# Second feed-forward stage of an encoder layer: three plain pairs instead of four, groups of 3, 6, 6 and 7 columns, and low parts made by DMA

## Chip, core and metric

The kernel runs on one core of one Trainium2 chip. The core has five engines that run their own instruction streams: TensorE (PE in the profile; its weight loads are shown apart as PEld), VectorE (DVE), ScalarE (ACT), GpSimd (POOL) and SyncE (SP). DMA transfers are issued from the queues of SP, ACT and POOL. The metric is the device time of one execution in microseconds, lower is better.

## What is computed

One layer of an encoder on x of shape 512 x 1024, in float32: a half-step SwiGLU, a mixer (Fourier groups beside attention), a second half-step SwiGLU, a final norm.

```python
def swiglu(h, w_gate, w_up, w_down):
    return (jax.nn.silu(h @ w_gate) * (h @ w_up)) @ w_down
...
x = x + 0.5 * swiglu(rms_norm(x, ffn1_norm), ffn1_w_gate, ffn1_w_up, ffn1_w_down)
...
x = x + jnp.concatenate([f_out, a_out], axis=-1) @ w_out
x = x + 0.5 * swiglu(rms_norm(x, ffn2_norm), ffn2_w_gate, ffn2_w_up, ffn2_w_down)
return rms_norm(x, final_norm)
```

The inner width of both SwiGLUs is 2752: 21 blocks of 128 and a tail of 64. The change lies in the second one alone.

## The kernel before

**Precision.** TensorE multiplies in a rounded 32-bit format. To keep float32 accuracy, every operand is split into a high part (rounded, made by ACT) and a low part (what rounding left, made by DVE: `lows`, L71-72), and every product is three matmuls: high x high, high x low, low x high (`product`, L108-111).

**Layout.** x lies transposed, 8 blocks of 128 channels by 512 positions. A "pair" j is a block of 128 gate columns and the same block of up columns of the weights. A "column" is one of the two; column 2j is pair j's gate, 2j + 1 its up. The tail, 64 of each, is one column by itself ("t", column 42).

**Two ways to make a pair.** A *plain* pair (`gate`) is two columns, each 8 channel blocks x 3 matmuls of 128 x 512, 48 in all. It runs on the unscaled h; the norm's factor is multiplied in when the result is taken from PSUM (`evacuate`). A *seven* (`seven`) uses a Winograd scheme with halves of the channels, of the positions, and of gate and up: seven products of quarter size in place of eight. One pair is then 7 x 4 x 3 = 84 matmuls of 128 x 256. It needs sums and differences of weight quarters (`prepare`) and of h quarters (`operands`, made once per stage into `rt`, in four parts), again with high and low parts.

**Groups.** The pairs of a stage are made and used up in groups (L28). The first group holds the plain pairs and the tail. For each group, eight output chunks d follow: `down` multiplies the group's activations with the down weights into a PSUM bank, `residual` adds the bank to x. The sevens of a group run one pair ahead: while group g's sevens run, the first pair of group g+1 is made as well, and the last pair of the first group is evacuated after the first chunk has started (`rest`). There are seven places for activations (`at`). In the last group of stage two, the last three chunks are taken in two halves of the positions (`closing`), so that norm, scaling and output of the first half run beside the matmuls of the second.

**Order.** TensorE's and SP's instructions stand in the order in which the code issues them (`in_order`). The order on ACT, DVE and POOL is drawn up by a scheduler; each engine works through its own queue strictly in that order.

**Buffers.** In the plain columns, high and low parts lie in `ring` slots and, lent for that time, in two free places of `at`: six slots, three columns at a time. Slots whose first columns alone are rewritten are let go as soon as those columns have been read. Raw weights are loaded by SP into three `raw` tiles.

**Low parts by DMA.** `rest_by_dma` (L90-93) makes a low part in another way: ACT writes minus the high part into the low tile, and a DMA from POOL's queue adds the source to it, from DRAM for weights, from the tile b for h. In stage one (`n_` is 0), the plain columns after the opening and the parts 2 and 3 of h are made so; in stage two (`n_` is 2) DVE makes all.

```python
    def rest_by_dma(lo, hi, src):
        nc.scalar.activation(lo, asf(hi), AF.Copy, scale=-1.0)
        nc.gpsimd.dma_start(out=lo, in_=src, accum_op=ALU.add)
```

**Start of stage two.** Columns 0 and 1 and the tail column come first, then the columns left, 2 to 7, one `gate` call each. Between them stand the evacuations that are due and the four calls of `operands` (L440-455).

Of the kernel before, what the change touches and what calls it, by code (L numbers as in the profile page):

```python
# [16 lines left out]
KD = D // P  # L17
# [7 lines left out]
FILL_LEAD = 0.1  # L25
NS = 12

GROUPS = ((0, "t", 1, 2), range(3, 9), range(9, 15), range(15, 21))  # L28
PLACES = 7
HALF = S // 2  # L30
USES = "a11", "a12", "s1", "s2", "s4", "s3", "a22"
# [11 lines left out]
def encoder(ctx, tc, A, out):  # L43
# [8 lines left out]
    def bank(name):  # L52
        return pp.tile([P, S], F32, tag="bank", name=name)
# [10 lines left out]
    def in_order():  # L64
        return tc.manual_schedule(engines={mybir.EngineType.PE, mybir.EngineType.SP})
# [5 lines left out]
    def lows(lo, src, hi):  # L71
        nc.vector.tensor_tensor(out=lo, in0=src, in1=asf(hi), op=ALU.subtract)  # L72
# [17 lines left out]
# [5 lines that stand above are left out]
    def weights(src, name, n=KD, raw=None, by_dma=False):  # L95
        raw = raw or raw_tile(src, name, n)
        hi, lo = weight_slots()
        if name in HI_DVE:
            nc.vector.tensor_copy(hi[:, :n, :], raw[:, :n, :])
        else:  # L100
            nc.scalar.copy(hi[:, :n, :], raw[:, :n, :])  # L101
        if by_dma:
            rest_by_dma(lo, hi, src)
        else:
            lows(lo[:, :n, :], raw[:, :n, :], hi[:, :n, :])
        return hi, lo

    def product(ps, whi, wlo, mhi, mlo, first, last):  # L108
        nc.tensor.matmul(ps, whi, mhi, start=first, stop=False)  # L109
        nc.tensor.matmul(ps, whi, mlo, start=False, stop=False)  # L110
        nc.tensor.matmul(ps, wlo, mhi, start=False, stop=last)  # L111
# [93 lines left out]
            nc.scalar.copy(self.rb[:, t], pss[1][:, t])  # L205
            return pss[0]

    def ffn(norm, after, wgu, wd, wdt, opening, closing):

        n_ = norm.n
        n_plain = len(GROUPS[0])
        with tc.tile_pool(name=f"act{n_}", bufs=1) as ap, tc.tile_pool(name=f"sums{n_}", bufs=2) as sp:
            at = ap.tile([P, PLACES, 2, S], F32R, name=f"at{n_}")
            rt = ap.tile([P, 7, 2, KH, HALF], F32R, name=f"rt{n_}")
# [3 lines left out]
            def place(j):  # L221
                where[j] = free.pop(0)
                return where[j]
# [3 lines left out]
            def gate(c, between={}, by_dma=False):  # L227
                whi, wlo = weights(wgu[c], f"gu{n_}_{c}", by_dma=by_dma)
                ps = bank(f"gu{n_}_{c}")
                for k in range(KD):  # L230
                    between.get(k, int)()
                    product(ps, whi[:, k, :], wlo[:, k, :], hh[k], hl[k], k == 0, k == KD - 1)
                return ps
# [18 lines left out]
            def operands(rp, i0, i1):  # L252
                for i in range(i0, i1):
                    b = sp.tile([P, 4, HALF], F32, tag="raw_g", name=f"b{n_}_{i}")
                    for o, k in ((0, i), (2, i + KH)):
                        nc.vector.scalar_tensor_tensor(
                            out=b[:, o : o + 2].rearrange("p a b -> p (a b)"), in0=x[k],
                            scalar=gains[:, norm.n, k : k + 1], in1=rp, op0=ALU.mult, op1=ALU.mult,
                        )
                    b12, b11, b22, b21 = (b[:, o] for o in range(4))  # L260
                    t = sp.tile([P, 4, HALF], F32, tag=("s12", "s34")[i % 2], bufs=1, name=f"t{n_}_{i}")
                    for o, (p, q) in enumerate(((b12, b11), (b22, t[:, 0]), (b22, b12), (b21, t[:, 1]))):
                        nc.vector.tensor_tensor(out=t[:, o], in0=p, in1=q, op=ALU.subtract)
                    for src, c in ((b[:, 1:], slice(0, 3)), (t, slice(3, 7))):
                        h, l = rt[:, c, 0, i], rt[:, c, 1, i]
                        nc.scalar.copy(h, src)
                        if src is t or i < 2 or n_:
                            lows(l, src, h)
                        else:
                            rest_by_dma(l, h, src)  # L270

            def back(ts):
                plain[:] = [t for t in plain if all(t is not q for q in ts)]
# [149 lines left out]
            def residual(d, ps, t):  # L423
                nc.vector.scalar_tensor_tensor(  # L424
                    out=x[d][:, t], in0=ps[:, t], scalar=0.5, in1=x[d][:, t], op0=ALU.mult, op1=ALU.add
                )

            every = slice(0, S)
            for gi, group in enumerate(GROUPS):
                last = gi == len(GROUPS) - 1  # L430
                ahead = []
                if gi:
                    rest = seven(range(group[0] + 1, min(group[-1] + 2, NF)), ready)
                else:
                    lent = [at[:, i].rearrange("p a b -> p (a b)") for i in range(PLACES - 4, PLACES)]
                    plain.extend(lent)
                    row = []
                    pss = dict(enumerate(opening(gate, lambda: norm.column([norm.acc]), lambda: row.append(norm.row()))))
                    back(lent[:2])
                    due, parts, left = [*pss, "t"], list(range(KH)), range(2 * len(pss), 2 * n_plain)  # L440
                    pss["t"] = [gate(2 * NF)]
                    tail_weights()
                    for i, c in enumerate(left):
                        pss.setdefault(c // 2, []).append(gate(c, by_dma=not n_))
                        if due:
                            j = due.pop(0)
                            evacuate(at[:, place(j)], n_, pss[j], norm)
                        if c % 2 and c != left[-1]:
                            due.append(c // 2)
                        while len(parts) * len(left) > (len(left) - 1 - i) * KH:  # L450
                            o = parts.pop(0)
                            operands(row[0], o, o + 1)

                    def rest():
                        evacuate(at[:, place(n_plain - 1)], n_, pss[n_plain - 1], norm)

                def added(d, ps):
                    residual(d, ps, every)
                    if last:
                        (after.sums if closing else after.add)(d)  # L460
                    if ahead:
                        f, *a = ahead.pop(0)
                        f(*a)

                waiting = []
                for d in range(KD):
                    if last and closing and d == KD - 3:
                        closing([(e, down(e, group, gi)) for e in range(d, KD)], residual)
                        break
                    if last and d == KD - 2:  # L470
                        back(lent)
                    ps = bank(f"dn{n_}_{d}_{gi}")
                    steps = down(d, group, gi)(ps, every)
                    for _ in range(len(group) - (last and d < 2)):
                        next(steps)
                    waiting.append((d, ps, steps))
                    if d == 1 and not last:
                        ready = prepare(GROUPS[gi + 1][0] + 1)
                        ahead.extend(ready[1])
                    if d == 0:  # L480
                        rest()
                        if last:

                            lent = slots[KD - 2 : KD]
                            plain[2:2] = lent
                            continue
                    for d_, ps, steps in waiting:
                        for _ in steps:
                            pass
                        added(d_, ps)  # L490
                    waiting = []
                for f, *a in ahead:
                    f(*a)
                if not gi:
                    back(lent)
                free.extend(where[j] for j in group)
# [34 lines left out]
    n0, n1 = Norm(0), Norm(1)  # L531
# [69 lines left out]
        return [pss[0:2], pss[2:4]]  # L601

    with in_order():
        ffn(n0, n1, A["wgu1"], A["wd1"], A["wdt1"], opening1, None)


    n2 = Norm(2)
# [378 lines left out]
    n3 = Norm(3)  # L986

    ready = (2, 3)
# [67 lines left out]
        finish(2, 4, n3.rows)  # L1056

    with in_order():
        ffn(n2, n3, A["wgu2"], A["wd2"], A["wdt2"], lambda gate, column, row: [[gate(0, {KD - 1: column}), gate(1, {3: row})]], closing)


def _order():
# [106 lines left out]
```

## Time and profile before

| | us |
|---|---|
| median of 3 runs | 876.37 |
| lowest and highest | 875.76, 877.21 |
| the profiled execution | 877.47 |
| its span, first to last instruction | 875.7 |
| stage two: first gate to the last matmul of the closing | 522.0 to 865.9 |
| of it, plain columns 2 to 7 | 540.0 to 572.9 |
| the first group's output chunks | 572.9 to 593.4 |
| three blocks of sevens, each with the chunks of its group | 593.4 to 687.1, to 781.0, to 865.9 |
| norm, scaling and output of the last half | 865.9 to 875.7 |

The profile is of one execution. In the lists of it, a row has a start, a length, the engine, the line of the kernel, the operation, output and input by the program's names (buffer numbers left out) and a count; in brackets stands how long the engine had been idle before it and what ended that. A matmul's listed length reaches from its start to its result, so rows of matmuls overlap; the step between starts is what one costs.

The granted clock of TensorE was 0.996 over the whole span.

### The profile page before, as it was taken

What the parts mean: (1) busy time and instruction counts of PE and PEld (TensorE: products, weight loads), DVE (VectorE), ACT (ScalarE), POOL (GpSimd) and SP (SyncE); (2) the same over time, 40 slices, a digit from 0 to 9 for tenths busy, and PEclk for the clock granted to TensorE, in tenths of its full rate; (3) what the DMA queues carried; (4) which work ended last, traced back from release to release, by engine and by line L of the source; (5) the groups of instructions that cost most, each with busy time, mean ns of one, the idle gap of its engine ahead of it and who ended that gap; (6) DMA issues with size and microseconds to landing.
All of it is one profiled execution on the core that took longest, in us unless ns stands there. A gap on an engine that the chain in (4) does not pass through costs nothing.

```text
span 875.7 us, 13587 instructions
## 1 busy us (share of the span) xinstructions
PE 862.0 (98%) x5391; PEld 769.1 (88%) x5391; DVE 640.8 (73%) x1011; ACT 459.0 (52%) x763; POOL 27.8 (3%) x33
## 2 busy tenths in 40 slices
PE   8999999999999999999999999999999999999996
PEld 6788998899989998888888888889998999889986
DVE  7798985488746837699888558987974698559554
ACT  7663664266524644677776445535652366226541
POOL 0110000000000000211000000000000000000001
PEclk9999999999999999999999999999999999999999
DMA  7664322323243113621110224242323232323212
GB/s 263 154 150 149 133 85 73 115 97 120 78 140 108 49 51 109 205 79 43 49 49 25 77 70 142 85 133 97 109 79 127 75 117 99 97 101 104 73 37 97
DMA packets 30609, 88.46 MB, mean 101 GB/s; under 512 B 3665, under 2 KB 8529, under 8 KB 30417
## 3 DMA queue, kind: packets, MB, share of 16 engines
q1 hardware_dynamic: 28304, 82.87, 28.3%
q0 software_dynamic: 1696, 4.20, 2.4%
q8 instruction: 42, 0.69, 0.3%
q10 hardware_dynamic: 544, 0.52, 0.2%
q14 instruction: 23, 0.18, 0.1%
HBM read 83.91 MB, written 2.10 MB: 98 GB/s over the span
## 4 chain that ended last, share of the span: by engine, by line
PE 94%; ACT 2%; DVE 2%; DMA 1%; issue 1%; SPq 0%; POOL 0%; DVEq 0%; ACTq 0%
PE r L338 22%; PE q L338 11%; PE dn L109 8%; PE dn L111 8%; PE dn L110 8%; PE p L338 6%; PE gu L109 3%; PE gu L111 3%; PE gu L110 3%; PE out L109 2%; PE out L111 2%; PE out L110 2%; PE pt L851 1%; PE q L109 1%; PE q L110 1%; PE q L111 1%
## 5 line engine op out<-in xcount | busy, mean ns | idle before, releaser
L338 PE MATMUL r<-rt,ring 128*128 128x256 f32 x1632 | 213.0, 282 | 0.0
L338 PEld LDWEIGHTS r<-rt,ring 128*128 128x128 f32 x1632 | 201.8, 188 | 2.4
L109 PE MATMUL dn<-at,ring 128*128 128x512 f32 x303 | 119.7, 395 | 0.0
L110 PE MATMUL dn<-at,ring 128*128 128x512 f32 x303 | 119.6, 395 | 0.0
L111 PE MATMUL dn<-at,ring 128*128 128x512 f32 x303 | 119.6, 395 | 0.0
L338 PE MATMUL q<-rt,ring 128*128 128x256 f32 x816 | 107.9, 281 | 0.0
L424 DVE SCALAR_TENSOR_TENSOR gx<-dn,gx 128x512 f32<-128x512 f32 x61 | 42.1, 690 | 82.0 <-PE dn L111 82.0
L338 PEld LDWEIGHTS q<-rt,ring 128*128 128x128 f32 x816 | 101.6, 188 | 0.0
L72 DVE TENSOR_TENSOR ring<-s,ring 128x1024 fp32r<-128x1024 f32 x68 | 82.9, 1221 | 17.8 <-PE r L338 10.9
L101 ACT CAST ring<-raw_dn 128x768 fp32r<-128x768 f32 (+1 forms) x59 | 45.5, 775 | 92.9 <-PE dn L110 78.8
L299 ACT CAST ring<-s 128x1024 fp32r<-128x1024 f32 x68 | 71.4, 1050 | 38.1 <-PE r L338 18.4
L111 PEld LDWEIGHTS dn<-at,ring 128*128 128x128 f32 x303 | 56.9, 188 | 13.8 <-DVE ring L72 0.2
L110 PEld LDWEIGHTS dn<-at,ring 128*128 128x128 f32 x303 | 57.0, 188 | 13.1
L109 PEld LDWEIGHTS dn<-at,ring 128*128 128x128 f32 x303 | 56.9, 188 | 13.0
L72 DVE TENSOR_TENSOR ring<-raw_dn,ring 128x768 fp32r<-128x768 f32 (+1 forms) x59 | 51.8, 881 | 7.2 <-ACT ring L101 6.2
L72 DVE TENSOR_TENSOR ring<-raw_g,ring 128x1024 fp32r<-128x1024 f32 x34 | 41.6, 1224 | 17.7 <-PE p L338 10.7
L338 PE MATMUL p<-rt,ring 128*128 128x256 f32 x408 | 54.0, 281 | 0.0
L338 PEld LDWEIGHTS p<-rt,ring 128*128 128x128 f32 x408 | 50.8, 188 | 0.0
L299 ACT CAST ring<-raw_g 128x1024 fp32r<-128x1024 f32 x34 | 35.7, 1049 | 22.2 <-DMA raw_g<-in_wgu 9.0
L308 ACT CAST ring<-raw_u 128x512 fp32r<-128x512 f32 x34 | 21.1, 621 | 39.3 <-PE dn L111 19.9
L383 DVE TENSOR_TENSOR u<-g,u 128x512 f32<-128x512 f32 x34 | 23.4, 688 | 15.9 <-ACT u L382 15.9
L109 PE MATMUL gu<-ring 128*128 128x512 f32 x80 | 31.3, 392 | 0.0
(328 smaller groups left out, 1579.9 us busy)
## 6 DMA issues: line engine op xcount, KB each, us to landing
raw_dn<-in_wd SPq DMA_DIRECT2D x48, 384.0 KB, 3.1
raw_g<-in_wgu SPq DMA_DIRECT2D x34, 512.0 KB, 3.8
raw_u<-in_wgu SPq DMA_DIRECT2D x34, 512.0 KB, 4.4
raw_gu<-in_wgu SPq DMA_DIRECT2D x14, 512.0 KB, 3.5
raw_o<-in_wo SPq DMA_DIRECT2D x8, 512.0 KB, 3.6
raw_dn<-in_wd SPq DMA_DIRECT2D x16, 192.0 KB, 2.4
raw_in<-in_wins SPq DMA_DIRECT2D x6, 512.0 KB, 3.6
raw_f<-in_winf SPq DMA_DIRECT2D x4, 512.0 KB, 3.8
```

Source lines behind the costliest of these rows:

```text
L72: nc.vector.tensor_tensor(out=lo, in0=src, in1=asf(hi), op=ALU.subtract)
L101: nc.scalar.copy(hi[:, :n, :], raw[:, :n, :])
L109: nc.tensor.matmul(ps, whi, mhi, start=first, stop=False)
L110: nc.tensor.matmul(ps, whi, mlo, start=False, stop=False)
L111: nc.tensor.matmul(ps, wlo, mhi, start=False, stop=last)
L299: nc.scalar.copy(hi, src)
L308: nc.scalar.copy(hi, src)
L338: nc.tensor.matmul(ps, a[:, ks], b[:, i], start=first and i == 0 and o == 0, stop=i == KH - 1 and o == 2, skip_group_check=not first,)
L383: nc.vector.tensor_tensor(out=u, in0=b["g"], in1=u, op=ALU.mult)
L424: nc.vector.scalar_tensor_tensor(out=x[d][:, t], in0=ps[:, t], scalar=0.5, in1=x[d][:, t], op0=ALU.mult, op1=ALU.add)
L851: nc.tensor.transpose(pt[:, c * P : (c + 1) * P], prob[t, b, c][:, kc * P : (kc + 1) * P], ident)
```

## The change

The list of groups is now a parameter of `ffn`, with a list for each stage. Stage one keeps its own. In stage two, the first group has pairs 0, t and 1 and makes pair 2 ahead by plain products; pair 3, plain before, is made by a seven. The groups after it are 2 to 7, 8 to 13 and 14 to 20, so the last has seven columns. Both conditions that kept `rest_by_dma` to stage one are dropped: in stage two, the low parts of columns 2 to 5 (gate and up weights of pairs 1 and 2) and of the parts 2 and 3 of h taken from b are made by ACT and DMA instead of DVE.

```diff
-GROUPS = ((0, "t", 1, 2), range(3, 9), range(9, 15), range(15, 21))
+GROUPS1 = ((0, "t", 1, 2), range(3, 9), range(9, 15), range(15, 21))
+GROUPS2 = ((0, "t", 1), range(2, 8), range(8, 14), range(14, 21))
...
-    def ffn(norm, after, wgu, wd, wdt, opening, closing):
+    def ffn(norm, after, wgu, wd, wdt, groups, opening, closing):
...
-        n_plain = len(GROUPS[0])
+        n_plain = len(groups[0])
...
                         nc.scalar.copy(h, src)
-                        if src is t or i < 2 or n_:
+                        if src is t or i < 2:
                             lows(l, src, h)
                         else:
                             rest_by_dma(l, h, src)
...
-            for gi, group in enumerate(GROUPS):
-                last = gi == len(GROUPS) - 1
+            for gi, group in enumerate(groups):
+                last = gi == len(groups) - 1
...
-                        pss.setdefault(c // 2, []).append(gate(c, by_dma=not n_))
+                        pss.setdefault(c // 2, []).append(gate(c, by_dma=True))
...
-                        ready = prepare(GROUPS[gi + 1][0] + 1)
+                        ready = prepare(groups[gi + 1][0] + 1)
...
-        ffn(n0, n1, A["wgu1"], A["wd1"], A["wdt1"], opening1, None)
+        ffn(n0, n1, A["wgu1"], A["wd1"], A["wdt1"], GROUPS1, opening1, None)
...
-        ffn(n2, n3, A["wgu2"], A["wd2"], A["wdt2"], lambda gate, column, row: [[gate(0, {KD - 1: column}), gate(1, {3: row})]], closing)
+        ffn(n2, n3, A["wgu2"], A["wd2"], A["wdt2"], GROUPS2, lambda gate, column, row: [[gate(0, {KD - 1: column}), gate(1, {3: row})]], closing)
```

## The prediction

> **What bounds the kernel now.** I read the page first: busy time, then the chain that ended last.
>
> ```profile
> span 875.7 us, 13587 instructions
> PE 862.0 (98%) x5391; PEld 769.1 (88%) x5391; DVE 640.8 (73%) x1011; ACT 459.0 (52%) x763; POOL 27.8 (3%) x33
> ...
> PE 94%; ACT 2%; DVE 2%; DMA 1%; issue 1%; SPq 0%; POOL 0%; DVEq 0%; ACTq 0%
> ```
>
> TensorE is busy all the time and is 94% of the chain. So the change is worth the TensorE time that it takes out, less any wait that it puts in. Next I cut the second feed-forward stage into stretches (columns: stretch, its length, then busy time and instructions of PE, PEld, DVE, ACT, POOL; granted clock; DMA share; GB/s).
>
> ```profile
> 556.45:567.35 10.90, 10.90 (x50) 9.01 (x48) 9.91 (x19) 5.73 (x8) 0.00 (x0) 1.00 0.31 97
> 567.35:572.94 5.59, 5.59 (x26) 4.52 (x24) 5.39 (x8) 2.60 (x4) 0.00 (x0) 1.00 0.28 105
> 572.94:593.37 20.43, 20.43 (x89) 16.55 (x88) 15.62 (x25) 6.66 (x10) 0.00 (x0) 1.00 0.43 142
> 593.37:652.15 58.78, 58.78 (x494) 58.56 (x492) 50.12 (x72) 35.40 (x61) 0.00 (x0) 1.00 0.29 100
> 781.01:829.82 48.81, 48.81 (x409) 48.59 (x408) 37.57 (x54) 28.08 (x49) 0.00 (x0) 1.00 0.28 88
> ```
>
> The rows are: plain columns 5 and 6 (two columns), plain column 7, the first group's eight output chunks, the first block of sevens (six of them without the last product), the last block (five of them, likewise). PE is busy for every length, at granted clock 1.00: there is no gap to win or to hide in. DVE is nearly full in the plain columns (5.39 of 5.59).
>
> **The change, part by part.** *Pair 3 is no longer plain.* Its columns are 6 and 7: half of 10.90 is 5.45, and 5.59, so 11.04 us of TensorE go. Bounds: two columns at the cheaper price, 10.90, or at the dearer, 11.18.
>
> *One more seven in the last block.* Six against five cost 58.78 - 48.81 = 9.97. The upper bound is the step from one seven to the next where a wait is in it, 10.10 (in the chain, the second product starts at 603.63 and 613.73). I take 9.97, since it is what one more costs a block.
>
> *Output chunks.* Three matmuls per chunk, 24 in all, move from the first group to the last. Out go 24 x 20.43/88 = 5.57. In come 15 whole ones at 0.2331 (in the block before, 126 take the 29.37 from 657.77 to 687.14) = 3.50, and 9 that the closing splits in halves, 18 at 0.119 (twelve take 1.43 in the chain) = 2.14. Together +0.07. Their weights move from 192 KB to 128 KB a chunk and from 384 to 448 KB: the bytes are the same, and SP issues as many loads as before.
>
> *Low parts by DMA.* DVE loses four lows of 1.22 and two of 0.95 for columns 2 to 5 and h, and ACT gains four negations of 1.06 and two of 0.85, POOL six issues (0.88 each for weights, 1.29 for h, from the first stage, where the same lines run). None of it is TensorE's, so its price is nothing as long as the lows land before TensorE asks. What hides them is the plain column before. These are the rows for the first, column 2, and for the same step in the first stage.
>
> ```profile
> 530.95 1.05 ACT L101 CAST ring<-raw_gu 128x1024 fp32r<-128x1024 f32 x1 [0.34 <-ACT wt L246]
> 531.90 0.58 ACT L194 COPY rb<-rp 128x512 f32<-128x512 f32 x1
> ...
> 539.96 0.39 PE L109 MATMUL gu<-ring 128*128 128x512 f32 x1
> 540.19 0.40 PE L110 MATMUL gu<-ring 128*128 128x512 f32 x1
> 540.42 0.39 PE L111 MATMUL gu<-ring 128*128 128x512 f32 x1
> ```
>
> ```profile
> 26.28 1.06 ACT L92 ACTIVATE ring<-ring 128x1024 fp32r<-128x1024 f32 x1
> 27.65 1.11 POOL L93 DMA_DIRECT2D ring<-in_wgu  x1 [1.22 <-ACT ring L92]
> ...
> DMA to landing us min/median/max: 5.2/5.7/7.5
> ```
>
> In the program's order the negation comes after the copy to rb: it starts at 532.43 and ends at 533.49. POOL starts 0.31 after such an end (27.34 to 27.65), at 533.80. Call the landing time x: the low is there at 533.8 + x. L111 is the first to use it, at 540.42, its weight load 0.19 earlier, so 540.2: room up to x = 6.4. Behind the negation on ACT stand the table load, the first silu and the cast of column 3; that column's negation ends near 538.1, POOL issues at 538.4, asked for at 545.7: room 7.3. Column 4 has some 8. Column 5 is the tight one again: ahead of its negation ACT now has the negation for h, a cast of h and a cast of the first output weights, and on POOL the DMA for h is issued first; added up from the rows, ACT ends it at 549.4, POOL issues at 549.7, asked for at 556.7: room 7.0. The median 5.7 fits all of them; 7.5, which one of four weight rows shows (the first, issued while 0.75 of the DMA time was taken; here it is 0.26), does not. I take 0 us; the bounds are 0 and, at 7.5, 1.1 + 0.5 = 1.6. The h lows are asked for only at the first seven, some 20 us later. SP's loads come no later than before: a raw tile is now let go after its cast, where it had to wait for DVE.
>
> The Trainium skill ("DMA: Bandwidth & Descriptors", section Anatomy of one DMA) has for a DMA issued from GpSimd about 2.0 us and bytes over 436 GB/s: 3.2 us here as an estimate. By it no low is ever late; the rows are 2 us and more above it, so I go by them.
>
> *The tail.* The last group has seven columns, so in the closing each half chunk has three more matmuls.
>
> ```profile
> 861.13 0.70 POOL L179 TENSOR_TENSOR r<-ms,mhalf 128x2 f32<-128x2 f32 x1 [332.05 <-DVE ms L172]
> ...
> 861.36 0.42 DVE L424 SCALAR_TENSOR_TENSOR gx<-last,gx 128x256 f32<-128x256 f32 x1 [0.31 <-PE last L111]
> 861.86 0.30 DVE L184 COPY wide<-r 128x256 f32<-128x256 f32 x1
> ...
> 862.22 0.43 PE L192 MATMUL rp<-ident,wide 128*128 128x128 f32 x2
> ```
>
> The transposes at L192 stay at the ninth step, and DVE keeps its order: the residual, then the copy to wide. But the residual now waits for the seventh step instead of the sixth, 0.36 later (861.72), so wide starts near 862.06, is there at 862.36, and TensorE waits about 0.2. Bounds 0 and 0.3. After the last matmul nothing is changed: that residual starts as soon as TensorE is done, as before.
>
> Sum: -11.04 + 9.97 + 0.07 + 0.20 = -0.80 us, on the profiled execution's own 877.47 (span 875.7 and 1.8 around it) 876.7; it is 1.1 above the median of three, 876.37, from which I get **875.6**. With the bounds of the prices 875.1 to 876.5.
>
> **Rivals.** *Late lows, slower.* The place is column 2 and, because column 5's cast waits for column 2's end, column 5 again: the stall is (x - 6.4) + (x - 7.0). For it: only 0.7 us of room, the room is worked out from sums of rows, and the first such DMA in this kernel took 7.5. Also on POOL's queue, larger and mixed loads took up to 9.4 (page, part 6). Against it: the three later ones, 5.2 to 5.7, with DVE full. At 7.5 it is 1.6: 877.2. It becomes slower than before by over 0.2% from x = 8.0; halfway between 7.5 and 9.4, at 8.45, it is 3.5: 879.1.
>
> The Trainium skill ("SBUF — State Buffer", section SBUF: two separate sides) says that DVE in a two-port mode, such as an f32 copy, locks GpSimd out of writing descriptors. As a mechanism here it is this rival: at 533.8 DVE runs the four products b of L256 and subtractions, not copies. At 34.74 such an issue beside them took 0.88 and landed after 5.6, so the trace speaks against it, and its chance is within the rival's.
>
> *DVE in the short first group.* Its chunks shrink from 20.43 to 14.86 us, and DVE's 15.62 there shrinks by only some 1.0 (eight lows of 256 instead of 384 columns). With 2.4 of pair 2's evacuation falling into it, 17.0 against 14.86 could hold up weights of a later chunk by 2.1: 877.7. Against it: about 3 us of that work prepare the second seven, which isn't asked for until 8.6 us into the block.
>
> *More gain, faster.* Three times per block a seven loses some 0.14, because a copy on ACT comes late:
>
> ```profile
> 610.75 2.98 PE r L338 x24
> ...
> 640.92 2.84 PE r L338 x24
> ```
>
> Were these nine waits and the tail's gone, it would be 1.2 + 0.2 more: 874.2. For it: ACT's order around the new groups is drawn up anew. Against it: the same three waits stand in every block of both stages, and nothing eases ACT.
>
> **Chances.** The sum holds 0.47. Late lows with x up to 8.0, 0.08; beyond, 0.24. DVE in the first group 0.05. More gain 0.16. Within 0.2% (1.75 us, about what a measurement of this kernel can tell from no change) lie the first, the mild late lows and the third: same 0.60; slower 0.24, faster 0.16. The range 874.0 to 879.2 holds the faster case and the milder half of the slower.
>
> **What would show it.** PE busy through the plain columns with no gap at the third matmul of columns 2 and 5; 21.9 us for columns 2 to 5, 14.9 for the first chunks, 58.8 for the last block; a wait of 0.2 before L193's transposes. A gap of 1 us or more at a plain column's first low, ended by a DMA of POOL's queue, would prove the sum wrong in favour of late lows; a gap within the first chunks ended by DVE, in favour of the third case; blocks under 58.5, of the fourth.

## The result and the profile after

The changed kernel is slower: 878.21 us (median of 22 runs, 876.46 to 881.31) against 877.41 for the kernel before measured beside it, a ratio of 1.0015 with a 95% interval of 1.0008 to 1.0021. Measured a second time, the same kernel gave 1.0027 (1.0017 to 1.0037). The forecast was a gain of 0.8 us; this is a loss of 0.8, small but clear of the interval. The profiled execution took 879.21, its span is 877.4. Lines of the changed kernel are those of the kernel before plus one from L28 on.

First the page of the changed kernel: span, busy times, and the chain that ended last.

```profile
span 877.4 us, 13713 instructions
PE 861.9 (98%) x5436; PEld 770.7 (88%) x5436; DVE 638.9 (73%) x1012; ACT 467.1 (53%) x776; POOL 34.0 (4%) x39
...
PE 86%; DMA 4%; DVE 3%; ACT 3%; issue 2%; SPq 0%; POOL 0%; DVEq 0%; ACTq 0%; POOLq 0%
```

PE's busy time is what it was (861.9 against 862.0). But PE's share of the chain fell from 94% to 86%: the end now hangs on DMA, DVE and ACT in places. Where, the stretches of stage two show (columns as in the prediction: stretch, length, busy time and count of PE, PEld, DVE, ACT, POOL, granted clock, DMA share, GB/s). The rows are columns 2 and 3, columns 4 and 5, the first chunks, the first block of sevens, the last block.

```profile
539.20:550.62 11.42, 11.20 (x50) 8.93 (x49) 11.33 (x19) 11.25 (x15) 3.03 (x3) 1.00 0.78 136
550.62:561.66 11.04, 11.04 (x50) 9.03 (x48) 8.32 (x14) 7.04 (x11) 1.27 (x1) 1.00 0.91 212
561.66:577.10 15.44, 15.29 (x65) 11.88 (x64) 12.41 (x22) 5.39 (x9) 0.00 (x0) 1.00 0.47 135
577.10:637.56 60.46, 59.17 (x494) 58.62 (x492) 53.56 (x78) 35.80 (x62) 0.00 (x0) 1.00 0.31 106
766.31:825.16 58.85, 58.85 (x493) 58.64 (x492) 45.99 (x66) 34.86 (x60) 0.00 (x0) 1.00 0.29 93
```

The last block, now with six sevens and the next group's none, takes 58.85 where five took 48.81: the added seven costs what it should. The first chunks take 15.44 where 14.86 was forecast, the first block 60.46 instead of 58.78, the four columns together 22.46 where an undisturbed run of them takes 21.94 (the experiment with the tail's column, below).

The opening of the kernel varies by over 2 us between executions (the first block of sevens of stage one begins at 80.25 before, at 79.61 after, and between 77.8 and 80.6 in the runs below), so I compare stage two alone: from the second half of gate column 1 (527.66 before, 526.89 after) to the start of the last matmul (869.40 and 870.62). That is 341.74 before and 343.73 after, 1.99 more. The sum had said 0.80 less. The 2.79 between them are column 2 (0.49), the chunks (0.58), the first block (1.68) and 0.04 elsewhere. Each was read from the matmuls' starts: a step between two of them, less the usual 0.233.

*Column 2.* The rows of PE there, POOL's issue, and the same transfer in the chain.

```profile
539.20 0.39 PE L110 MATMUL gu<-ring 128*128 128x512 f32 x1
539.43 0.40 PE L111 MATMUL gu<-ring 128*128 128x512 f32 x1
540.05 0.50 PE L112 MATMUL gu<-ring 128*128 128x512 f32 x1 [0.22 <-DMA ring<-in_wgu]
```

```profile
532.98 0.93 POOL L94 DMA_DIRECT2D ring<-in_wgu  x1 [4.67 <-ACT ring L93]
...
532.98 7.02 DMA ring<-in_wgu
```

The third matmul, the first to use the low part, starts 0.62 after the second. The transfer was issued 6.22 ahead of the column, as forecast (6.16), but took 7.0 and not the median of 5.7.

*Chunks.* ACT and DVE at the end of the columns and in the first chunks of the changed kernel (in brackets the idle time before, and what ended it).

```profile
558.99 1.05 ACT L300 CAST ring<-raw_g 128x1024 fp32r<-128x1024 f32 x1 [3.25 <-DMA raw_g<-in_wgu]
...
560.07 1.23 DVE L73 TENSOR_TENSOR ring<-raw_g,ring 128x1024 fp32r<-128x1024 f32 x1 [1.84 <-ACT ring L300]
...
566.36 1.22 DVE L73 TENSOR_TENSOR ring<-s,ring 128x1024 fp32r<-128x1024 f32 x1
567.49 0.42 DVE L73 TENSOR_TENSOR ring<-raw_dn,ring 128x256 fp32r<-128x256 f32 x1
567.83 0.68 DVE L425 SCALAR_TENSOR_TENSOR gx<-dn,gx 128x512 f32<-128x512 f32 x1
568.43 1.22 DVE L73 TENSOR_TENSOR ring<-s,ring 128x1024 fp32r<-128x1024 f32 x1
569.56 0.42 DVE L73 TENSOR_TENSOR at<-raw_dn,at 128x256 fp32r<-128x256 f32 x1
```

The weights of the first seven (raw_g) come late, ACT and DVE sit idle for them, and then DVE works without a break to 573.4. In its queue the long low parts of the seven's sums (566.36, 568.43) stand ahead of the low parts of down weights 3 and 4 (567.49, 569.56), and PE's gaps are where these two are used: the matmuls that wait for them start at 567.96 and 570.03.

*First block.* SP's loads of the changed kernel and then DVE and ACT.

```profile
553.33 0.33 SPq L292 DMA_DIRECT2D raw_g<-in_wgu  x1
...
554.69 15.64 SPq L88 DMA_DIRECT2D raw_dn<-in_wd  x6
570.43 0.38 SPq L292 DMA_DIRECT2D raw_g<-in_wgu  x1
571.54 0.33 SPq L292 DMA_DIRECT2D raw_u<-in_wgu  x1
...
583.25 0.33 SPq L292 DMA_DIRECT2D raw_g<-in_wgu  x1
583.63 0.42 SPq L292 DMA_DIRECT2D raw_u<-in_wgu  x1
```

```profile
577.75 0.69 DVE L315 TENSOR_TENSOR s<-raw_u 128x512 f32<-128x512 f32 x1 [3.47 <-DMA raw_u<-in_wgu]
```

```profile
588.06 0.62 ACT L309 CAST ring<-raw_u 128x512 fp32r<-128x512 f32 x1 [3.86 <-DMA raw_u<-in_wgu]
588.59 1.04 ACT L300 CAST ring<-raw_g 128x1024 fp32r<-128x1024 f32 x1
589.53 0.36 ACT L375 COPY u<-r 128x256 f32<-128x256 f32 x1
```

This reads as a relay. SP's queue stands on the loads of down weights, whose tiles come free late; so the second seven's weights are issued at 570.43 and 571.54, and raw_u is there 0.65 after the block has begun (577.75), DVE being idle for 3.47. That sets when the tiles come free for pair 6 (583.25, 583.63), and ACT's cast of its raw_u waits until 588.06. Behind that cast, in ACT's strict order, stands the copy at 589.53 that frees a bank, and PE waits for it 1.2 us: the list of PE's waits gives it.

```profile
PE r L339 <- ACT u L375: 1.2, 1, 1.2
PE gu L112 <- DMA ring<-in_wgu: 0.2, 1, 0.2
```

### The profile page after: what moved, and what is told of

Read it like the earlier page. It is cut to its first block, busy times and chain, and to the rows that moved or that the text cites. A ratio compares the mean times of both kernels' runs of the same rounds, so it can differ in the third digit from the quotient of the medians.

```text
span 877.4 us, 13713 instructions
## 1 busy us (share of the span) xinstructions
PE 861.9 (98%) x5436; PEld 770.7 (88%) x5436; DVE 638.9 (73%) x1012; ACT 467.1 (53%) x776; POOL 34.0 (4%) x39
## 4 chain that ended last, share of the span: by engine, by line
PE 86%; DMA 4%; DVE 3%; ACT 3%; issue 2%; SPq 0%; POOL 0%; DVEq 0%; ACTq 0%; POOLq 0%
PE r L339 21%; PE q L339 10%; PE dn L110 8%; PE dn L111 8%; PE dn L112 8%; PE p L339 5%; DMA raw_u<-in_wgu 2%; PE out L110 2%; PE out L112 2%; PE gu L112 2%; PE out L111 2%; PE gu L111 2%; PE gu L110 2%; PE pt L852 1%; PE q L110 1%
## 5 line engine op out<-in xcount | busy, mean ns | idle before, releaser
L339 PE MATMUL r<-rt,ring 128*128 128x256 f32 x1680 | 219.4, 283 | 1.4 <-ACT u L375 1.2
L339 PEld LDWEIGHTS r<-rt,ring 128*128 128x128 f32 x1680 | 207.7, 188 | 4.2 <-ACT u L375 1.4
L339 PE MATMUL q<-rt,ring 128*128 128x256 f32 x840 | 111.1, 281 | 0.0
L339 PEld LDWEIGHTS q<-rt,ring 128*128 128x128 f32 x840 | 104.6, 188 | 0.0
L73 DVE TENSOR_TENSOR ring<-s,ring 128x1024 fp32r<-128x1024 f32 x70 | 85.4, 1221 | 19.0 <-PE r L339 12.4
L300 ACT CAST ring<-s 128x1024 fp32r<-128x1024 f32 x70 | 73.5, 1050 | 37.5 <-PE r L339 17.2
L102 ACT CAST ring<-raw_dn 128x768 fp32r<-128x768 f32 (+3 forms) x58 | 45.3, 784 | 90.2 <-PE dn L111 74.8
L73 DVE TENSOR_TENSOR ring<-raw_dn,ring 128x768 fp32r<-128x768 f32 (+3 forms) x58 | 51.6, 893 | 6.0 <-ACT ring L102 4.0
L309 ACT CAST ring<-raw_u 128x512 fp32r<-128x512 f32 x35 | 21.7, 621 | 41.5 <-DMA raw_u<-in_wgu 16.9
L846 ACT ACTIVATE e<-s,mx,sc 128x512 f32<-128x512 f32 x32 | 25.1, 786 | 11.4 <-DVE mx L844 11.2
```

What stands on the lines that cost most here:

```text
L300: nc.scalar.copy(hi, src)
L309: nc.scalar.copy(hi, src)
L339: nc.tensor.matmul(ps, a[:, ks], b[:, i], start=first and i == 0 and o == 0, stop=i == KH - 1 and o == 2, skip_group_check=not first,)
L846: nc.scalar.activation(e, ps, AF.Exp, bias=mx, scale=f, accum_out=zs[t][:, c, b : b + 1])
```

## The experiments

Theory at the outset: the terms of TensorE were right, and what went wrong is the low parts by DMA, those of h above all, whose transfers hold the tiles b (one tag with raw_g) and lie beside the first seven's loads. Rivals: the shorter first group by itself is too short for DVE; or only the slow landing at column 2 matters. In each diff a minus line is the changed kernel's.

**Halves of the change.** The new groups with all low parts by DVE (`e1_groups_only`), and the old groups with the low parts by DMA (`e2_dma_only`: one list of groups for both stages again).

```diff
-                        if src is t or i < 2:
+                        if src is t or i < 2 or n_:
...
-                        pss.setdefault(c // 2, []).append(gate(c, by_dma=True))
+                        pss.setdefault(c // 2, []).append(gate(c, by_dma=not n_))
```

> The new groups alone: low parts of columns 2 to 5 and of h stay with VectorE. Theory A (the first output chunks, shortened from 20.4 to 14.9 us, are too short for the preparation of the next sevens, so that weight loads come late and a cast that waits for one holds up ScalarE): VectorE has 6.8 us more to do in the same time, so the waits in the chunks and in the first block grow; +2 to +5 us on the kernel before. Theory B (the accumulating DMAs are what costs: the first lands late, and the tile of h that they hold keeps the first weight load back): without them the change is worth the sum of TensorE's terms, -0.8 us.

> The low parts by DMA alone, in the kernel before with its old groups (columns 2 to 7 and parts 2 and 3 of h). Theory A: only column 2's low is late, some 0.4 us, the chunks still have 20.4 us: 0 to +0.5 us on the kernel before, first block of sevens 58.8 us. Theory B: the lost time is here too: +1.5 to +2.5 us.

Neither half is better than the whole: 1.0068 (1.0056 to 1.0080) and 1.0039 (1.0025 to 1.0053), both more than either theory had allowed for. In the first, the chunks lose 6.5 us. PE's waits there, and two stretches:

```profile
PE dn L112 <- DVE ring L73: 3.1, 1, 3.1
PE dn L110 <- ACT ring L102: 1.4, 1, 1.4
```

```profile
566.80:570.03 3.23, 0.16 (x1) 0.00 (x1) 3.23 (x6) 0.00 (x0) 0.00 (x0) 1.00 0.00 0
570.03:573.49 3.46, 3.46 (x9) 2.72 (x10) 3.04 (x5) 2.54 (x4) 0.00 (x0) 0.52 0.39 114
```

DVE is busy through the whole of PE's wait: without the DMAs the short first group is too short for DVE. So the DMAs are needed by the new groups, and h's and the columns' must not be judged alike. In the second, columns 2 and 6 wait for their low parts, 1.0 and 1.6, with landings of 6.9 to 9.4 (one of h's 4.4) where several are under way together; no block is disturbed but the last, by 0.3.

**Which low parts.** Column 2's by DVE (`e4_col2_dve`), and h's by DVE with the columns' left to DMA (`e8_h_dve`, the first two lines of the diff above).

```diff
-                        pss.setdefault(c // 2, []).append(gate(c, by_dma=True))
+                        pss.setdefault(c // 2, []).append(gate(c, by_dma=not n_ or c > 2))
```

> The changed kernel with the low part of column 2 made by VectorE again, the other three columns and h by DMA. Theory A: only the 0.4 us wait at column 2's third matmul goes, and VectorE is 1.2 us later, so that some of it may come back in the chunks: +0.7 to +1.3 us on the kernel before. Theory B: column 5's low follows column 2's, so both are repaired: -0.3 to +0.3 us.

> The changed kernel with h's low parts by VectorE, columns 2 to 5 by DMA. Theory A (VectorE and the weight loads in a first group that is too short): VectorE has 1.9 us more to do before the chunks, the waits in them grow by about that: +2 to +4 us on the kernel before. Theory B for h (the tile b is held until its DMA lands, 4.4 to 7 us, and the first raw gate weights wait for it): the first load is issued earlier than 24 us before the first seven, the waits in chunks and first block shrink: 0 to +0.6 us.

`e4` has no gap at column 2, but loses 1.8 in the chunks, where DVE is 1.2 later and the first seven's load is issued only at 557.39: 1.0031 (1.0019 to 1.0043), more than either theory had priced. `e8` gives DVE 1.9 more and yet has clean chunks and a clean block (58.83); only column 2 still waits, 0.6: 0.9998 (0.9989 to 1.0007). That seemed to fit the theory. The first seven's loads land in 3.6 and 4.5 us instead of 5.6 and 6.5. The answers on DMA issues, first of the changed kernel, then of `e8` (the last number is us from issue to landing):

```profile
raw_g<-in_wgu SPq DMA_DIRECT2D x1, 512.0 KB, 5.6
raw_u<-in_wgu SPq DMA_DIRECT2D x1, 512.0 KB, 6.5
```

```profile
raw_g<-in_wgu SPq DMA_DIRECT2D x1, 512.0 KB, 3.6
raw_u<-in_wgu SPq DMA_DIRECT2D x1, 512.0 KB, 4.5
```

The Trainium skill ("DMA: Bandwidth & Descriptors", section Queues, rings and completion order) says that each DMA engine serves the queues that have work in turn, a packet at a time; the 2 us that SP's loads lose beside POOL's transfer agree with that.

Yet what these 2 us cost isn't shown. The changed kernel issues raw_g 8.3 us ahead of the first chunk and has it 2.8 ahead; `e8` issues it 6.7 ahead and has it 3.1 ahead. Against the chunks, the slow load is there only 0.3 later.

**Earlier loads.** A third tile for raw_g and b (`e3_third_tile`), paid for with single tiles of `kept`; and these single tiles alone, as a control (`e7_single_kept`).

```diff
-                    b = sp.tile([P, 4, HALF], F32, tag="raw_g", name=f"b{n_}_{i}")
+                    b = sp.tile([P, 4, HALF], F32, tag="raw_g", bufs=3 if n_ else 2, name=f"b{n_}_{i}")
...
-                g = sp.tile([P, KD * P], F32, tag="raw_g", name=f"raw_g{n_}_{j}")
+                g = sp.tile([P, KD * P], F32, tag="raw_g", bufs=3 if n_ else 2, name=f"raw_g{n_}_{j}")
...
-                    t = sp.tile([P, HALF], F32, tag=n, name=f"{n}{n_}_{j}")
+                    t = sp.tile([P, HALF], F32, tag=n, bufs=1 if n_ and n != "u2" else 2, name=f"{n}{n_}_{j}")
```

> The changed kernel with a third tile for raw gate weights (and the tiles b of h) in stage two, paid for by one instead of two buffers for the kept products p1 and p5. Theory A: the loads of the first pairs no longer wait for a tile; the first block of sevens goes from 60.5 to 58.8 us and the first chunks from 15.4 to 14.9: -0.8 to 0 us on the kernel before, some 2 less than the changed kernel. Theory B's first half (column 2's low): only what it does not touch stays, 0.4 us at column 2. If the seven itself or the DMA traffic is what costs: no change from the changed kernel, +1.3.

> A control: the changed kernel with one instead of two buffers for the kept products p1 and p5, and no third tile. If the third tile is what removed the waits, this has them still: first block of sevens 60 us or more, +1 to +2.5 us on the kernel before. If it was the buffers' effect on the schedule, the first block is 58.8.

`e3` issues the first seven's load at 541.39 instead of 553.33, and the stalls of chunks and first block are gone; column 2 still waits 0.24. Its stretches: columns 2 and 3, 4 and 5, chunks, first block (the cut before the chunks lies 0.12 early, in column 5).

```profile
537.92:549.10 11.18, 11.18 (x49) 8.93 (x48) 11.06 (x20) 10.91 (x15) 2.90 (x3) 1.00 1.05 236
549.10:560.02 10.92, 10.92 (x49) 8.95 (x48) 10.29 (x19) 6.89 (x11) 1.43 (x2) 1.00 0.62 114
560.02:574.89 14.87, 14.87 (x67) 12.11 (x66) 13.49 (x23) 5.62 (x10) 0.00 (x0) 1.00 0.56 202
574.89:633.66 58.77, 58.77 (x493) 58.55 (x492) 50.74 (x74) 35.46 (x61) 0.00 (x0) 1.00 0.27 92
```

From its first matmul on, the chunks take 14.75, as in every run without a stall there; the block takes 58.77. Stage two takes 340.96, 0.78 less than before. That this is the forecast sum to 0.02 is in part luck, since the sum had no wait at column 2. The timing, 1.0000 (0.9992 to 1.0009), neither shows nor excludes such a gain. The control keeps the stalls (first block 59.85): 1.0021 (1.0012 to 1.0030).

**What is left.** On top of the third tile, column 2's low part by DVE and the tail column's by DMA (`e5_tail_column`); then also the closing's norm one step later (`e6_later_norm`, run twice).

```diff
-                    pss["t"] = [gate(2 * NF)]
+                    pss["t"] = [gate(2 * NF, by_dma=n_ > 0)]
...
-                if i == 5:
+                if i == 6:
...
-                if i == 9:
+                if i == 10:
```

> The kernel with the third tile, and the low by DMA moved from column 2 to the tail column, which is asked for some 10 us after its cast; VectorE makes column 2's low, so its work is the same. If the first accumulating DMA of a stage lands after 6.8 to 8 us wherever it stands, as all runs so far show, the tail column's is there in time and column 2's wait of 0.25 us goes: no gap in the plain columns, -0.9 to -0.2 us on the kernel before. If what was late at column 2 was its place in ScalarE's order, the same. If the accumulate's time is what counts in sum (traffic), nothing moves against the run with the third tile alone (0.0, interval -0.7 to +0.8).

> The same, and in the closing the norm's column of the first half at step 6 instead of 5 and its rows at step 10 instead of 9. By the prediction's step on the tail, the wait of 0.2 us before the transposes goes and nothing takes its place: the gap at their line falls from 0.29 to 0.12 us between starts, 0.2 us faster than the run before it. If VectorE's six scalings then run past the last matmul, 0.1 to 0.4 slower instead.

> The same kernel as e6_later_norm, on the same chip as the two beside it, to compare them in one call: 0.9989 of before, within 0.9980 to 0.9997.

Stage two takes 340.71 and 340.79 (again: 340.62), with no gap in columns, chunks or blocks. The ratios are 0.9990 (0.9980 to 1.0001), 0.9989 (0.9980 to 0.9997) and 0.9994 (0.9985 to 1.0002). The later norm removes the wait at the transposes (0.14 and 0.12 between starts instead of 0.29), but the timing shows nothing of it: `e5` and `e6` do not differ. In the profiles, up to the last transposes, `e6` is 0.26 and 0.09 shorter than `e5`; 0.34 of the 340.79 are these transposes at a lower clock (last section). The tail column's transfer has nothing that waits for it soon and landed after 5.4 to 5.7. So the first such transfer of a stage isn't slow wherever it stands, as `e5`'s expectation had it; `e4`'s had landed after 5.5 already.

**Does DVE for h replace the third tile?** `e9_no_third_tile` is `e6` without the third tile and with h by DVE; `e10_h_dve_too` keeps the tile.

> e6_later_norm with the third tile and the single kept tiles taken back, and the low parts of h by DVE instead of DMA; the low part of the tail column and of columns 3 to 5 by DMA, of column 2 by DVE. My theory: the third tile and DVE for h cure the same thing (the first weight loads are neither late nor slow), so the time is that of e6: 875.2, ratio to before 0.9985 to 0.9995, no stall in the chunks, first block 58.8. Rival: the third tile gave something of its own, or DVE, with 1.9 us more work per stage and column 2's low as well, is late in the first group's chunks (column 2's low alone cost e4 about 1 us there): 876.2 or more, ratio above 1.0, gaps in the chunks ended by DVE.

> e6_later_norm, third tile kept, but the low parts of h by DVE. My theory: with a third tile the accumulates of h cost TensorE nothing, so taking them away gives nothing: 875.2, within 0.3 of e6. Rival one: they still slow the loads beside them, then it is 0.3 or more faster than e6. Rival two: DVE is nearly full in the columns and its 1.9 us more make it late in the chunks: 0.5 or more slower than e6.

It does not: `e9` loses 1.2 in the chunks, at the low part of a down weight, though h has no DMA and the loads land in 3.6 and 4.6: 1.0009 (1.0000 to 1.0019), with `e6` beside it at 0.9994. So the theory in its first form fell: DVE can be late there without any of h's DMAs. `e10` is 1.0002 (0.9993 to 1.0012), with 0.3 lost in the block, within the timing's reach of `e6`.

**DVE's order against h's DMAs.** `e8` differs from the changed kernel in a second way. Its drawn-up DVE order has the low parts of down weights 3 and 4 ahead of the seven's long ones. Both were separated by writing the order of the first group out by hand: `e11` has h by DMA with the order of `e8`, `e12` h by DVE with the order of the changed kernel. In the string, W is a chunk's weights, p a piece of `prepare`, g a residual.

```diff
+                    with tc.manual_schedule(engines={mybir.EngineType.PE, mybir.EngineType.SP, mybir.EngineType.DVE}):
+                        for a in "p0 p1 p5 p4 W2 p2 g0 W3 g1 p6 W4 p3 g2 W5 g3 p7 W6 g4 W7 g5 g6 g7".split():
```

> The changed kernel, h's low parts by DMA as in it, but in the first group of stage two the order of DVE's work is written out by hand, and it is that of e8_h_dve: the low parts of down weights 3 and 4 stand ahead of the low parts of the first seven's sums, where the changed kernel has them behind. Column 2's wait (about 0.5) and the tail's (0.17) stay. Theory A, the order decides (what e8 cured by moving h back to DVE it cured through another drawn-up order): no stall in the chunks, first block near 58.8, stage two 2.3 shorter than in the changed kernel, some 875.9, ratio 0.999 to 1.0005. Theory B, the accumulates of h decide (they share the DMA engines with the first weight loads): the stalls of 0.6 and 1.7 stay, ratio 1.0010 to 1.0021.

> The mirror of it: e8_h_dve (h's low parts by DVE) with the DVE order of the changed kernel in the first group of stage two. Theory A, the order decides: the stalls in the chunks and the first block come back, 2 or more in all, ratio 1.001 to 1.003. Theory B, the accumulates decide: they stay away, chunks 14.9, first block 58.8, ratio 0.999 to 1.0007.

Time lost in the profiles, chunks / first block:

| | h by DMA | h by DVE |
|---|---|---|
| order of the changed kernel | 0.6 / 1.7, again 1.0 / 1.0 | 1.0 / 0.1 (`e12`) |
| order of `e8` | 0.0 / 1.5, again 0.0 / 1.4 (`e11`) | 0.0 / 0.05 (`e8`) |

Neither theory is the whole. The chunks' loss goes with the order, and in this table the first block's goes with h's DMAs. (`e12` loses a further 0.5 in its second block.) But one load sorts the first block's losses better. It is raw_u of the second seven, issued while the chunks run. Here are all profiles of the new groups with two tiles:

| | raw_u lands, us from the block's start | the block loses |
|---|---|---|
| changed kernel, again | +0.6, -0.1 | 1.7, 1.0 |
| `e11`, again | +0.3, +0.1 | 1.5, 1.4 |
| `e7` | -0.7 | 1.1 |
| `e4` (h by DMA too) | -1.2 | 0.05 |
| `e12`, `e9`, `e8`, `e1` (h by DVE) | -1.6, -1.7, -1.8, -2.1 | 0.1, 0.0, 0.05, 0.1 |

In the first three rows this load took 4.9 to 6.4 us, in the others 4.0 to 5.0. h's transfers had landed over 16 us before the block, so none of them lies beside it. Nor is `e11` equal to `e8` in all but h: the order written out leaves out the evacuation of pair 2, whose last low part (`at<-u2p`) stands ahead of a down weight's in `e11` and behind it in `e8`, and raw_u is issued 5.9 and 6.3 us before the block instead of 6.8. How h's DMAs make this load late is thus not shown; `e4` has them and loses nothing.

The timing of `e11`, 0.9989 (0.9980 to 0.9999), did not fit its profile; `e12` had 1.0007 (0.9998 to 1.0016). So the changed kernel and `e11` were run again side by side, with `e13_all`: `e6` with the order of `e8`.

> The changed kernel once more, beside e11's kernel on the same chip. If the hand-written order is worth what the two earlier calls say, the ratio is 1.001 to 1.002 again, with stalls of some 0.6 in the chunks and 1.7 in the first block in this execution too.

> The kernel of e11_order_of_e8 once more: its timing (0.9989) and its one profile (a stall of 1.5 left in the first block) said different things. If the stall belongs to h's DMA and stands in most executions, the ratio is 1.0000 to 1.0012 and the profile shows it again, with the chunks clean. If it comes in some executions only, the ratio is below 1.0 again and the profile may be without it.

> e6_later_norm (third tile, column 2's low part by DVE and the tail column's by DMA, norm of the closing one step later) with the DVE order of e8 in the first chunks. With a third tile nothing is late, so the order should give nothing more: within 0.3 us of e6, ratio 0.9985 to 0.9997. If DVE's order still cost something there, 0.5 or more below e6, under 0.9985.

The changed kernel came out at 1.0027 (1.0017 to 1.0037) and `e11` at 1.0014 (1.0005 to 1.0022). The second profile of `e11` is as the first. Its chunks, its first block, and a row of its ACT:

```profile
560.40:575.26 14.86, 14.86 (x67) 12.09 (x66) 12.25 (x22) 5.41 (x9) 0.00 (x0) 1.00 0.51 173
575.26:635.48 60.22, 59.29 (x494) 58.73 (x493) 53.63 (x78) 35.89 (x62) 0.00 (x0) 1.00 0.29 98
```

```profile
585.88 0.62 ACT L313 CAST ring<-raw_u 128x512 fp32r<-128x512 f32 x1 [3.52 <-DMA raw_u<-in_wgu]
```

The chunks are clean (14.75 from their first matmul on), the block still loses 1.4 at the same late raw_u of pair 6 (L313 here is L309). So the order is worth about 1.1 us (0.0013 in the ratio, though the intervals overlap a little), and the late load of the second seven, by the profiles, 1.4. `e13`, 0.9993 (0.9985 to 1.0002), is no better than `e6`: with a third tile, the order no longer counts. Its raw_u lands late as well, 0.1 before the block, and the block loses only 0.2: pair 6's weights, which don't wait for a tile now, are issued 3 to 4 us before the block and not 6 us into it.

The same kernel differed by up to 0.0025 in the ratio from one measurement to the next (`e11`), more than one interval spans. I therefore trust differences between kernels measured side by side, and the profiles' losses, which came out alike twice in `e11`, less so in the changed kernel (0.6 and 1.7, then 1.0 and 1.0).

Five runs (`e5`, `e6` twice, `e13`, and `e11` once) have ratios of 0.9989 to 0.9994. Stage two of `e5`, `e6` and `e13` is 1.0 us shorter than before in all four profiles. That is a gain at the edge of what can be timed, not a safe one.

## Why the prediction was wrong

**TensorE's terms were right to some 0.2 us.** Two plain columns less, one seven more, and the chunks moved: in `e5`, where the tail's wait is the only one left, stage two is 1.03 shorter, against a sum of -0.80. Its columns give -11.07 (forecast -11.04), its first chunks -5.68 (-5.57), its last block +10.03 (+9.97), its closing +5.89 (+5.84 with the tail's wait). Another 0.2 less stands in the groups between, which the change leaves alone. (The prediction's bounds of the prices, "875.1 to 876.5", don't add up: its terms give 875.2 to 875.9, and 877.5 with the late lows' 1.6.) The tail's wait was 0.17 where 0.20 was forecast, at the place named: the residual at 861.71 (forecast 861.72), the copy to wide at 862.05 (862.06).

**The step that failed is "Low parts by DMA":** "None of it is TensorE's, so its price is nothing as long as the lows land before TensorE asks." Its price was 0; stage two lost 2.79 against the sum. Two parts of the step failed.

*The wrong user was watched.* I asked when TensorE needs each low part; h's are "asked for only at the first seven, some 20 us later", and that held. The larger loss, 2.3, came in elsewhere: at low parts of down weights that stand late in DVE's queue (chunks, 0.6 to 1.0), and through the late load of the second seven (first block, 1.0 to 1.7). Both are gone with a third tile (`e3`) and stay in its control (`e7`), so both hang on when raw tiles come free and loads start. h's transfers did slow the first seven's loads, from 3.6 and 4.5 us to 5.3 to 6.9. But that this leads to the first block's loss is argued, not shown: the block lost 1.0 to 1.7 in five profiles with h's DMAs, 0.0 to 0.1 in four without them (`e1`, `e8`, `e9`, `e12`), and 0.05 in `e4` with them. Why the second seven's load is late stays open.

*The landing of column 2.* Room 6.4 was right, and the bound of 7.5 was the row to take: over the runs with this transfer it landed after 6.6 to 7.6 and cost 0.1 to 1.0. "Here it is 0.26" was the DMA share of the kernel before. SP's loads of two later columns, freed by ACT's cast instead of DVE's, were issued at 530.18 and 531.26, the second 1.3 us earlier before column 2 than in the kernel before, and over the 7.0 us of this transfer the share was 0.82 with it, where the kernel before shows 0.31 in the same stretch. "No later than before" was true, and part of the harm. In `e9`, where column 2's low part is DVE's, the next transfer (column 3's) was issued at 535.66, with the column loads done, and took 5.5. That comparison is no experiment of its own.

**The third rival, DVE in the short first group, came closest**, and I gave it 0.05. Its price was 2.1; the chunks and the first block lost 2.3 here and 2.0 in the second profile. That the sums agree is partly luck, as its mechanism put all of it into the chunks, which lost 0.6 and 1.0. I had dismissed it since 3 us of DVE's work there "prepare the second seven, which isn't asked for until 8.6 us into the block". But TensorE's asking is not the date: SP's queue, the raw tiles and ACT's queue pass the delay on to pair 6, and PE stops 11.4 us into the block (588.5). Nor was DVE free to put that work last: its order put two low parts of 1.22 ahead of those that the chunks wanted. `e12` prices the order alone at 1.0.

**Late lows** had the place, column 2, and the mechanism, but 0.5 (1.0 in the second profile) is below the 1.6 it was priced at, and column 5 never waited. **More gain** did not come: blocks two and three took 58.99 and 58.85.

The range, 874.0 to 879.2, held because it was wide: the time moved the other way. The third rival's time of 877.7 is what the first ratio makes of 876.37.

## What to carry to other kernels

A transfer moved off a busy engine is not free because its own user comes late: list which loads it runs beside and whose tiles it holds, and ask what these loads feed. When a stage is made shorter, hold the engine behind TensorE against the new length with its queue order, not only with its sum, and follow a delay through tiles and queues to the next load. If such work must go to DMA, make the loads beside it early first: here one more tile took away all but 0.3 us of what the queue order, or moving the work back, cured only in some versions.

## What the runs showed of the hardware

Accumulating transfers of 384 and 512 KB from POOL's queue landed after 4.4 to 9.4 us; those of 512 KB with little beside them after 5.2 to 5.8.

In `e1` TensorE's granted clock was 0.52 for 3.46 us after a wait of 3.2, with 0.427 between matmuls instead of 0.233: eight such steps cost 1.6 us on top of the wait. After waits of up to 1.6 at columns, chunks and blocks in other runs the steps stayed at full clock. The last eight transposes of the kernel, all behind the same gap of 0.57, took 0.88 us from the first start to the last in most profiles, but 1.07 to 1.61 in `e1`, `e4`, the first of `e6` and the first of `e11`, where the granted clock was 0.80, 0.57, 0.71 and 0.54. The Trainium skill ("TensorE: Matmul & The Clock Gate", Part 1) gives one idle window of about 3.4 us as what halves the clock, and as much sustained work to bring it back; the 3.46 us agree with that, while the wait of 3.2 is a little shorter than its window. No run here shows why the transposes differ.
